# A two-layer hybrid network (SSD mixer, then MLA attention): three projection tiles in step with the input, and group 0's last steps moved into the next group's stream

## The chip, the cores and the metric

The kernel runs on one core of one Trainium2 chip. The metric is the device time of one execution in microseconds (us). A core has five engines that work from instruction streams of their own: PE (matrix products), DVE (vector operations), ACT (activations, copies), POOL and SP; here SP only issues DMAs, and POOL does nothing that matters. Within its stream an engine works in order: an instruction that waits for another engine holds up all that stands behind it.

## The reference

Sequence 512, width 1024, two layers with residuals, fp32. Layer 0 is an SSD (state space) mixer, layer 1 an MLA attention mixer:

```python
u = rms_norm(h, norm_w[0])
proj = u @ in_w                                  # 2048 z + 4096 xbc + 32 dt columns
xbc = silu(causal_depthwise_conv(xbc, conv_w, conv_b))      # 4 taps
dt = softplus(dt_raw + dt_bias);  a = -dt * exp(a_log)
# 8 groups of 4 heads, chunks of 128 tokens:
cb      = C_t . B_s                               # per group and chunk
y_diag  = (cb * exp(a_cum[t] - a_cum[s]), s <= t) @ (x * dt)
states  = B^T @ (x * dt * exp(a_end - a_cum));  carried over chunks
y_off   = (C @ entering_state) * exp(a_cum)
y = (y_diag + y_off + D * x) * silu(z)
h = h + (group_rms_norm(y) * norm_w) @ out_w
# layer 1: MLA mixer (low-rank q and kv, rope, 16 heads, gate silu(z)), then the final rms_norm
```

The change touches layer 0 alone.

## The kernel before

Everything is kept transposed, 128 channels on the partitions by 512 tokens. A product of full precision is made of three fp32r products: each operand is split into a high part (an ACT cast: `whi`, `vh`, `ah`) and the rest (a DVE subtraction: `wlo`, `vl`, `al`), and high by high, low by high and high by low are added in PSUM. So one projection tile (128 output channels) is 8 steps over the input channels of 3 products, 24 products of 128x512.

**Weights.** One tile's weights are 128x1024 fp32 (512 KB). SP loads them in the table's order into two `raw` buffers; ACT writes `whi`, DVE writes `wlo` (three buffers each). When a tile is asked for, the split of the tile after it has just been put into the streams (LOOK is 1).

**The first tiles.** The input x comes in 8 pieces of 256 KB, the first two weight tiles in quarters between them. `gemm2` (L300) makes the B and C tiles of group 0 together, step by step. These first products take x before its norm (`vh`, `vl`); the factor 1/rms comes from a sum of squares and two products with a matrix of ones (`pssq`, L356, L357), an Ln and an Exp on ACT, three DVE steps (`rr`), and it is multiplied in when the PSUM tiles are taken out (L606).

**Groups.** `ssm_in(g)` makes six tiles for group g: B, C, x0, x1, z0, z1 (called B1, C1 ... for group 1). Each is followed by its evacuation: for B, C and x an ACT pass (L608) and three DVE taps of the convolution (L610), and silu on ACT once all are there. The SSD work of a group has steps: `lexp` (four `L` rows are loaded from DRAM by SP, ACT and DVE subtract, ACT takes the exponent), `cb` (transposes of B, L71, and C by B, L77; the result is multiplied into the L tiles by DVE), `x(0)` and `x(1)` (transposes of x, L89, then `xdt` and `xw` on DVE), `states` (L105, then the carry `S` on DVE) and `y` (L130 into `yo`, L138 into `yd`, then DVE). There are four L buffers: the L rows of the next group are loaded when `yd` of this one has read them. `gnorm` is the gated norm of a group's y: squares, `pssq` products, Ln, Exp, DVE.

**What sets the order.** PE's stream is written out by hand: `sched` runs the six tiles of group g+1 and drops the steps of group g between them, at the positions of a table (in us of product time since the start of that stream): `P0` for group 0's steps in the stream of group 1, `P1` for all later ones, `GN` for the gated norm of the group before. The ACT and DVE streams are set by a scheduler that works on what PE's order asks for. On ACT, all uses of the exp/ln table (`E`) and of the silu table (`S`) are kept in phases that alternate; the table load stands between them, and a phase begins only when the one before it is through.

Of the kernel before, what the change touches and what calls it, by code (L numbers as in the profile page):

```python
# [15 lines left out]
P = 128  # L16
T = 512
# [19 lines left out]
S0P = (13.82, 14.2, 15.4, 15.6, 17.62)  # L37
SU = (0.64, 1.42)
P0 = (6.0, 6.8, 11.91, 15.25, 17.25, 24.88, 34.5)
# [12 lines left out]
SQ = 2  # L52

# [98 lines left out]
class Net:  # L152
# [123 lines left out]

    def mm(self, n=T):
        return self.ps.tile([P, n], F32, tag="mm", name=self.nm("mm"), bufs=3)
# [16 lines left out]
    def gemm2(self, ps, ws, xh, xl, ks):  # L295
        seqs = [self.passes(w, xh, xl, ks) for w in ws]
        for k in range(ks):
            for p, seq in zip(ps, seqs):
                for i in range(3 * k, 3 * k + 3):
                    self.nc.tensor.matmul(p, seq[i][0], seq[i][1], start=i == 0, stop=i == 3 * ks - 1)  # L300
            yield 6 * 0.216
# [35 lines left out]
    def sumsq(self, tiles, n, pstag, pool=None, tags=("r0", "rt", "rr"), after=None):  # L337
        nc = self.nc
        acc = None
        for x in tiles:  # L340
            sq = self.nrm.tile([P, T], F32, tag="sq", name=self.nm("sq"), bufs=SQ)
            i = nc.scalar.activation(sq[:], x, AF.Square)
            if after is not None:
                self.link(i, [after])
# [15 lines left out]
    def ssm(self):  # L360
# [10 lines left out]
        self.phase, self.group = "E", [self.head]  # L371
        raws = [self.wraw.tile([P, D], F32, tag="raw", name=self.nm("raw")) for _ in range(2)]
        self.wload = 2
        for k in range(KD):
            x = self.res.tile([P, T], F32, tag="res", name=self.nm("x"))
            nc.sync.dma_start(x[:], t["x"][k])
            self.xs.append(x)
            if k % 2 == 0:
                s = slice(k * P, (k + 2) * P)
                for i, raw in enumerate(raws):  # L380
                    nc.sync.dma_start(raw[:, s], t["w"][i, :, s])
# [11 lines left out]
        vh, vl = [], []  # L393
        ws = [self.split_weight(raw, (256, 512, 768)) for raw in raws]
        for k in range(KD):
            a = self.o16.tile([P, T], F32R, tag="o", name=self.nm("vh"))
            b = self.o16.tile([P, T], F32R, tag="o", name=self.nm("vl"))
            last = nc.scalar.activation(a[:], self.xs[k][:], AF.Copy, scale=nw[:, k:k + 1])
# [9 lines left out]
        self.wpos = 2  # L408
# [24 lines left out]
        for g in range(NG):  # L433
            ys, q = [], []
            pieces = [] if g == 0 else [(GN, late)]
            if g == 0:
                begin = lambda: q.append(SSD(self, 0, self.lexp(0), ys))
                pieces += [(SU[0] + SU[1] * k, scaled) for k in range(KD)]
                pieces += [(P0[0], step), (P0[1], step), (P0[1] + 0.1, begin)]
                at = P0[2:]  # L440
            else:
                q.append(SSD(self, g, self.lexp(g), ys))
# [122 lines left out]
    def ssm_in(self, g, uh, ul, early):  # L565
# [3 lines left out]
        for i, (name, ct) in enumerate((("B", 16 + g), ("C", 24 + g), ("x0", 2 * g), ("x1", 2 * g + 1),  # L569
                                        ("z0", 0), ("z1", 0))):  # L570
            pair = (0, 1) if g == 0 and i < 2 else (4, 5) if g == NG - 1 and i >= 4 else None
            w = None if pair and i == pair[1] else self.weight("w", U_IN + 6 * g + i)
# [5 lines left out]
            if pair:  # L578
                if i == pair[0]:
                    two = [ps, self.mm()]  # L580
                    ws = [w, self.weight("w", U_IN + 6 * g + i + 1)]
                    yield from self.gemm2([p[:] for p in two], ws, xh, xl, KD)
# [489 lines left out]
```

## Time and profile before

| | |
|---|---|
| median of 3 runs | 840.51 us (840.49 to 840.99) |
| the profiled execution | 840.15 us, span of its instructions 838.3 us |
| PE busy | 822.8 us (98%) |
| DVE busy | 640.2 us (76%) |
| ACT busy | 453.5 us (54%) |
| HBM read, written | 83.12 MB, 4.33 MB |

The span is what the profiler saw from the first instruction to the last; 1.85 us of the execution lie around it. In the rows, PE's products are pipelined: a row's length is longer than the distance to the next row, and the distance is the rate. An entry in square brackets is the idle time of the engine just before an instruction, and what ended it.

### The profile page before, as it was taken

Reading aid. Unit: us, or ns where it says so; the run is one execution under the profiler, and the core shown is the slowest. Engines: PE = TensorE matmul, PEld = TensorE weight load, DVE = VectorE, ACT = ScalarE, POOL = GpSimd, SP = SyncE. Lnnn points to the kernel's source line nnn. Section 1 sums busy time; section 2 is a strip of 40 time slices with the busy share of each in tenths; the row PEclk is TensorE's granted clock in tenths of the full one; section 3 lists DMA queues with packets and bytes.
Section 4 is the critical chain, followed back from the end, with each engine's and each line's share of the span. In section 5 each row is a group of like instructions: output and inputs, shape, how many; then the busy total and the mean of one; then the engine's idle time right before and its main releaser. Section 6 shows DMA issues by size and latency. Waiting matters only on the chain.

```text
span 838.3 us, 11586 instructions
## 1 busy us (share of the span) xinstructions
PE 822.8 (98%) x4260; PEld 694.8 (83%) x4260; DVE 640.2 (76%) x1226; ACT 453.5 (54%) x802; POOL 0.2 (0%) x4
## 2 busy tenths in 40 slices
PE   7999999999999999999999999999999999999996
PEld 5887888888888888888888888888888888888885
DVE  7899898979788979776564887786767869675544
ACT  7567755545565657333354664456547557554233
POOL 0000000000000000000000000000000000000000
PEclk9999999999999999999999999999999999999999
DMA  6354543434242424323225242222221224331212
GB/s 227 102 186 145 153 150 106 147 101 128 98 151 76 151 87 137 121 95 101 90 86 176 79 129 64 77 65 73 73 64 56 89 75 157 100 100 53 92 59 100
DMA packets 35112, 90.55 MB, mean 108 GB/s; under 512 B 4784, under 2 KB 6320, under 8 KB 35056
## 3 DMA queue, kind: packets, MB, share of 16 engines
q1 hardware_dynamic: 34336, 88.77, 32.9%
q10 hardware_dynamic: 720, 1.05, 0.3%
q8 instruction: 33, 0.54, 0.3%
q14 instruction: 23, 0.19, 0.1%
HBM read 83.12 MB, written 4.33 MB: 104 GB/s over the span
## 4 chain that ended last, share of the span: by engine, by line
PE 91%; DVE 5%; DMA 2%; ACT 1%; issue 1%; SPq 0%; DVEq 0%; ACTq 0%
PE mm L291 54%; PE ot L942 11%; PE s L794 5%; PE mm L300 4%; PE po L836 4%; PE mm L774 3%; PE pt L818 2%; PE yd L138 2%; PE yd L291 1%; PE aux L130 1%; PE aux L105 1%; DMA x<-in_x_dram 1%; PE aux L77 1%; PE aux L89 1%; DMA L<-ac_d 1%; DVE wlo L273 1%
## 5 line engine op out<-in xcount | busy, mean ns | idle before, releaser
L272 ACT CAST whi<-raw 128x1024 fp32r<-128x1024 f32 (+3 forms) x132 | 127.0, 965 | 214.7 <-PE mm L291 177.4
L273 DVE TENSOR_TENSOR wlo<-raw,whi 128x1024 fp32r<-128x1024 f32 (+3 forms) x132 | 146.8, 1115 | 56.1 <-ACT whi L272 55.8
L291 PE MATMUL mm<-ah,whi 128*128 128x512 f32 x384 | 153.9, 401 | 0.0
L291 PE MATMUL mm<-ah,wlo 128*128 128x512 f32 x384 | 150.1, 391 | 0.4 <-DVE wlo L273 0.4
L291 PE MATMUL mm<-al,whi 128*128 128x512 f32 x384 | 149.8, 390 | 0.0
L291 PE MATMUL mm<-vh,whi 128*128 128x512 f32 x224 | 89.6, 400 | 0.9 <-ACT whi L272 0.9
L291 PE MATMUL mm<-vh,wlo 128*128 128x512 f32 x224 | 87.8, 392 | 0.7 <-DVE wlo L273 0.7
L291 PE MATMUL mm<-vl,whi 128*128 128x512 f32 x224 | 87.5, 391 | 0.0
L291 PEld LDWEIGHTS mm<-ah,wlo 128*128 128x128 f32 x384 | 72.1, 188 | 16.0 <-DVE wlo L273 0.8
L291 PEld LDWEIGHTS mm<-ah,whi 128*128 128x128 f32 x384 | 72.2, 188 | 15.5 <-issue 1.4
L291 PEld LDWEIGHTS mm<-al,whi 128*128 128x128 f32 x384 | 72.2, 188 | 14.4 <-DVE al L312 0.3
L942 PE MATMUL ot<-whi,ah 128*128 128x512 f32 (+1 forms) x136 | 52.3, 384 | 0.0
L942 PE MATMUL ot<-whi,al 128*128 128x512 f32 (+1 forms) x136 | 51.4, 378 | 0.0
L942 PE MATMUL ot<-wlo,ah 128*128 128x512 f32 (+1 forms) x136 | 51.4, 378 | 0.0
L291 PEld LDWEIGHTS mm<-vh,wlo 128*128 128x128 f32 x224 | 42.0, 188 | 10.8 <-DVE wlo L273 1.5
L291 PEld LDWEIGHTS mm<-vh,whi 128*128 128x128 f32 x224 | 42.1, 188 | 9.2 <-ACT whi L272 1.1
L223 ACT ACTIVATE p<-p,st 128x128 f32<-128x128 f32 (+1 forms) x64 | 36.1, 564 | 25.1 <-DVE st L806 25.0
L291 PEld LDWEIGHTS mm<-vl,whi 128*128 128x128 f32 x224 | 42.2, 188 | 7.2
L822 ACT CAST ph<-pt 128x512 fp32r<-128x512 f32 (+1 forms) x64 | 26.5, 422 | 33.2 <-PE pt L818 32.8
L291 PE MATMUL mm<-ch,whi 128*128 128x512 f32 x104 | 42.6, 409 | 0.0
L291 PE MATMUL mm<-ch,wlo 128*128 128x512 f32 x104 | 40.8, 392 | 0.0
L291 PE MATMUL mm<-cl,whi 128*128 128x512 f32 x104 | 40.7, 392 | 0.0
(225 smaller groups left out, 1642.6 us busy)
## 6 DMA issues: line engine op xcount, KB each, us to landing
raw<-in_w_dram SPq DMA_DIRECT2D x100, 512.0 KB, 3.3
L<-ac_d SPq DMA_DIRECT2D x32, 256.0 KB, 3.8
E<-ea_d SPq DMA_DIRECT2D x32, 128.0 KB, 3.3
raw<-in_ua_dram SPq DMA_DIRECT2D x8, 512.0 KB, 3.3
raw<-in_ub_dram SPq DMA_DIRECT2D x8, 320.0 KB, 2.9
x<-in_x_dram SPq DMA_DIRECT2D x8, 256.0 KB, 4.3
res<-in_x_dram SPq DMA_DIRECT2D x8, 256.0 KB, 3.3
hd<-ht SPq DMA_DIRECT2D x8, 256.0 KB, 2.3
```

What stands on the lines that cost most here:

```text
L138: nc.tensor.matmul(yd[64 * h:64 * h + 64, s], self.xdt[j][:, c, h, :], self.L[2 * j + h][:, s], start=True, stop=True)
L223: i = self.nc.scalar.activation(out, in_, func, **k)
L272: nc.scalar.copy(hi[:, a:b], raw[:, a:b])
L273: nc.vector.tensor_tensor(lo[:, a:b], raw[:, a:b], hi[:, a:b].bitcast(F32), op=ALU.subtract)
L291: self.nc.tensor.matmul(ps, a, b, start=i == 0, stop=i == len(seq) - 1)
L300: self.nc.tensor.matmul(p, seq[i][0], seq[i][1], start=i == 0, stop=i == 3 * ks - 1)
L774: nc.tensor.matmul(ps[:, c2 * 256:(c2 + 1) * 256], a, b, start=i == 0, stop=i == 5)
L794: nc.tensor.matmul(ps[:, :n], x[:, s], y[:, :n], start=k == 0, stop=k == 4)
L818: nc.tensor.transpose(pt[:, (b - kb) * P:(b - kb + 1) * P], probs[h][b][:, kb * P:(kb + 1) * P], self.ident)
L822: nc.scalar.copy(ph[:, :n], pt[:, :n])
L836: nc.tensor.matmul(po[:, kb * P:], x, y, start=kb == 0 and k == 0, stop=kb == NCH - 1 and k == 2)
L942: nc.tensor.matmul(ps[:, a:b], x, y, start=start and i == 0, stop=stop and i == 5)
```

## The change

- Eight products of a zero matrix with itself (128x128, fp32) stand at the head of PE's stream; DVE clears the matrix first.
- Three weight tiles, not two, come in quarters with x: group 0's B, C and x0 are made together, step by step. The third tile's raw weights lie in two `act` buffers for that time. SP issues 12 quarters between the 8 pieces of x. The splits of the three tiles (`split_first`) stand between the casts of x.
- The squares of x for the norm are released one by one (after the cast of the piece three further on) and no more after the last cast.
- The four first steps of the table (dt products, norm, the multiplication by `rr`, evacuation) all stand behind the three tiles, at 15.5; the dt transposes follow the fourth tile.
- In the stream of group 1 (`ssm_in(1)`), group 0's steps stand later: `a4` 12.5 (6.0 before), `lexp` 14.1 (6.9), `cb` 19.4 (11.91), `x` 22.5 and 24.0 (15.25, 17.25). Its `states` and `y` (24.88 and 34.5 before) leave that stream: they are now at 2.0 and 7.0 of the stream that makes group 2's tiles, where group 1's own steps move back to 12.0 to 27.0 (1.0 to 18.2 before), and group 0's gated norm to 29.5 (16.84). From the stream of group 3 on the table is as it was.

```diff
-S0P = (13.82, 14.2, 15.4, 15.6, 17.62)
+S0P = (15.5, 15.51, 15.52, 15.53, 24.2)
-P0 = (6.0, 6.8, 11.91, 15.25, 17.25, 24.88, 34.5)
+P0 = (12.5, 14.0, 19.4, 22.5, 24.0)
+PL = (2.0, 7.0)
+PM = (12.0, 13.4, 14.8, 21.0, 27.0)
+GM = 29.5
+WARM = 8
...
+    def split_first(self, raw):
+        nc = self.nc
+        hi = self.whi.tile([P, D], F32R, tag="hi", name=self.nm("whi"))
+        lo = self.wlo.tile([P, D], F32R, tag="lo", name=self.nm("wlo"))
+        for k, part in enumerate(raw):
+            s = slice(2 * k * P, 2 * (k + 1) * P)
+            nc.scalar.copy(hi[:, s], part)
+            nc.vector.tensor_tensor(lo[:, s], part, hi[:, s].bitcast(F32), op=ALU.subtract)
+            yield
+        yield hi, lo
...
+        nc.vector.memset(idle[:], 0.0)
+        pw = aux()
+        for _ in range(WARM):
+            nc.tensor.matmul(pw[:, :P], idle[:], idle[:], start=True, stop=True)
         raws = [self.wraw.tile([P, D], F32, tag="raw", name=self.nm("raw")) for _ in range(2)]
+        third = [self.act.tile([P, T], F32, tag=g, name=self.nm("raw")) for g in ("ah", "al")]
...
-            pss = self.sumsq([x[:] for x in self.xs], D, "aux", after=last)
+            pss = self.sumsq([x[:] for x in self.xs], D, "aux", after=[marks[min(k + 3, KD - 1)] for k in range(KD)])
...
-            pieces = [] if g == 0 else [(GN, late)]
+            pieces = [] if g == 0 else [(GM if g == 1 else GN, late)]
+            elif g == 1:
+                pieces += [(PL[0], lambda: first[0].states()), (PL[1], lambda: first[0].y()), (PL[1] + 0.1, begin)]
+                at = PM
...
-            pieces += [(at[0], lambda: q[0].cb()), (at[1], lambda: q[0].x(0)), (at[2], lambda: q[0].x(1)),
-                       (at[3], lambda: q[0].states()), (at[4], lambda: q[0].y())]
+            pieces += [(at[0], lambda: q[0].cb()), (at[1], lambda: q[0].x(0)), (at[2], lambda: q[0].x(1))]
+            if g:
+                pieces += [(at[3], lambda: q[0].states()), (at[4], lambda: q[0].y())]
...
-            pair = (0, 1) if g == 0 and i < 2 else (4, 5) if g == NG - 1 and i >= 4 else None
+            pair = (0, 1, 2) if g == 0 and i < 3 else (4, 5) if g == NG - 1 and i >= 4 else None
```

Lines of the changed kernel are higher by 4 to 28 than those of the same code before. Three places of the streams that result:

PE's stream from its head, where the zero products now stand (`vh_`, `vl_` are the parts of x; `whi_`, `wlo_` with one number belong to one weight tile). Before:

```order
L300 MATMUL mm_184<-vh_130,whi_133 128x512
L300 MATMUL mm_184<-vl_131,whi_133 128x512
L300 MATMUL mm_184<-vh_130,wlo_134 128x512
L300 MATMUL mm_185<-vh_130,whi_137 128x512
L300 MATMUL mm_185<-vl_131,whi_137 128x512
L300 MATMUL mm_185<-vh_130,wlo_138 128x512
L300 MATMUL mm_184<-vh_142,whi_133 128x512
```

Now:

```order
L391 MATMUL aux_97<-idle 128x128 x8
L315 MATMUL mm_209<-vh_147,whi_150 128x512
L315 MATMUL mm_209<-vl_148,whi_150 128x512
L315 MATMUL mm_209<-vh_147,wlo_151 128x512
L315 MATMUL mm_210<-vh_147,whi_154 128x512
L315 MATMUL mm_210<-vl_148,whi_154 128x512
L315 MATMUL mm_210<-vh_147,wlo_155 128x512
L315 MATMUL mm_211<-vh_147,whi_158 128x512
L315 MATMUL mm_211<-vl_148,whi_158 128x512
L315 MATMUL mm_211<-vh_147,wlo_159 128x512
L315 MATMUL mm_209<-vh_163,whi_150 128x512
```

A step over the input channels is now nine products and not six.

DVE's stream ahead of the weights of tile B2, the first tile of group 2 (its `wlo` is 841 before and 849 now). Before:

```order
L94 TENSOR_TENSOR xw_645<-xdt_770,dec 128x3x128
L610 SCALAR_TENSOR_TENSOR x_132_731<-raw_732,cols,x_132_731 128x509
L606 TENSOR_TENSOR raw_786<-mm_752,rr_311 128x512
L273 TENSOR_TENSOR wlo_795<-raw_746,whi_794 128x1024
L109 COPY S_830<-aux_825 128x256
L610 SCALAR_TENSOR_TENSOR x_142_785<-raw_786,cols,x_142_785 128x511
L112 TENSOR_TENSOR S_832<-S_830,dec 128x256
L610 SCALAR_TENSOR_TENSOR x_142_785<-raw_786,cols,x_142_785 128x510
L113 TENSOR_TENSOR S_832<-aux_825,S_832 128x256
L610 SCALAR_TENSOR_TENSOR x_142_785<-raw_786,cols,x_142_785 128x509
L112 TENSOR_TENSOR S_835<-S_832,dec 128x256
L273 TENSOR_TENSOR wlo_841<-raw_792,whi_840 128x1024
```

Now:

```order
L638 SCALAR_TENSOR_TENSOR x_130_735<-raw_736,cols,x_130_735 128x511
L638 SCALAR_TENSOR_TENSOR x_140_790<-raw_791,cols,x_140_790 128x511
L638 SCALAR_TENSOR_TENSOR x_130_735<-raw_736,cols,x_130_735 128x510
L638 SCALAR_TENSOR_TENSOR x_140_790<-raw_791,cols,x_140_790 128x510
L638 SCALAR_TENSOR_TENSOR x_130_735<-raw_736,cols,x_130_735 128x509
L638 SCALAR_TENSOR_TENSOR x_140_790<-raw_791,cols,x_140_790 128x509
L96 TENSOR_TENSOR xdt_821<-aux_816,dt 128x512
L96 TENSOR_TENSOR xdt_835<-aux_830,dt 128x512
L98 TENSOR_TENSOR xw_728<-xdt_821,dec 128x3x128
L98 TENSOR_TENSOR xw_728<-xdt_835,dec 128x3x128
L277 TENSOR_TENSOR wlo_849<-raw_797,whi_848 128x1024
```

From the multiplication of the dt tile by `rr` (L500, now L528) to this row, DVE's stream holds the same instructions as before less four of group 0's carry `S` and one `wlo`, which stands ahead of `rr` now.

ACT's stream at the silu of group 2 (its B is 1013 before and 929 now; `r_210`, `r_230` are the Ln and Exp of group 0's gated norm). Before:

```order
L608 ACTIVATE C_1049<-mm_1024,cols 128x512
L353 CAST sqh_1125<-sqa_1118 128x512
L272 CAST whi_1209<-raw_1103 128x1024
L608 ACTIVATE x_199_1098<-mm_1060,cols 128x512
L223 ACTIVATE r_210_1132<-pssq_1129 128x512
L223 ACTIVATE r_210_1132<-r_210_1132 128x512
L232 ACT_TABLE_LOAD
L232 ACTIVATE B_1013<-B_1013 128x512
L232 ACTIVATE C_1049<-C_1049 128x512
```

Now:

```order
L660 ACTIVATE L_1300<-L_1300,ac 128x128
L660 ACTIVATE L_1300<-L_1300,ac 128x128 x3
L357 ACTIVATE sq_1497<-y_1238 128x512
L227 ACTIVATE r_230_1276<-pssq_1273 128x512
L357 ACTIVATE sq_1501<-y_1243 128x512
L227 ACTIVATE r_230_1276<-r_230_1276 128x512
L641 COPY z_233_1292<-mm_1199 128x512
L236 ACT_TABLE_LOAD
L236 ACTIVATE B_929<-B_929 128x512
L236 ACTIVATE C_1037<-C_1037 128x512
```

The Ln, Exp and silu of that phase now stand behind the last tile of group 2 and behind the first `L` row of group 2's own exponents (`L_1300`), which is loaded after group 1's `yd` products.

More of the change, by code (lines that the diff above doesn't have):

```diff
@@ L371, in ssm @@
         self.phase, self.group = "E", [self.head]
+        idle = wk.tile([P, P], F32, name="idle", bufs=1)
+        nc.vector.memset(idle[:], 0.0)
+        pw = aux()
+        for _ in range(WARM):
+            nc.tensor.matmul(pw[:, :P], idle[:], idle[:], start=True, stop=True)
         raws = [self.wraw.tile([P, D], F32, tag="raw", name=self.nm("raw")) for _ in range(2)]
-        self.wload = 2
+        raws = [[raw[:, 2 * k * P:2 * (k + 1) * P] for k in range(KD // 2)] for raw in raws]
+        third = [self.act.tile([P, T], F32, tag=g, name=self.nm("raw")) for g in ("ah", "al")]
+        raws.append([third[k // 2][:, (k % 2) * 2 * P:(k % 2 + 1) * 2 * P] for k in range(KD // 2)])
+        self.wload = 3
         for k in range(KD):
@@ L579, in ssm_in @@
                 if i == pair[0]:
[L580 to L581 removed]
+                    two = [ps] + [self.mm() for _ in pair[1:]]
+                    ws = [w] + [self.weight("w", U_IN + 6 * g + k) for k in pair[1:]]
                     yield from self.gemm2([p[:] for p in two], ws, xh, xl, KD)
```

23 lines of the change are left out of this document (12 added, 11 removed).

## The prediction

> **What bounds the kernel now.** First the page's span and busy times, then the list of what PE waited for, then PE's rows in order of time at its gaps.
>
> ```profile
> span 838.3 us, 11586 instructions
> PE 822.8 (98%) x4260; PEld 694.8 (83%) x4260; DVE 640.2 (76%) x1226; ACT 453.5 (54%) x802; POOL 0.2 (0%) x4
> ```
>
> PE, 98% busy, sets the time. Its waits after 90 us, the whole list, are two of 0.2 us:
>
> ```profile
> PE mm L291 <- ACT whi L272: 0.2, 1, 0.2
> PE mm L291 <- DVE wlo L273: 0.2, 1, 0.2
> ```
>
> So what is to be won lies before 90 us, and whatever the change makes PE wait later is new. PE's rows there:
>
> ```profile
> 4.77 0.80 PE L300 MATMUL mm<-vh,whi 128*128 128x512 f32 x1 [4.77 <-ACT whi L272]
> ...
> 7.99 0.63 PE L300 MATMUL mm<-vl,whi 128*128 128x512 f32 x1
> 8.42 0.63 PE L300 MATMUL mm<-vh,wlo 128*128 128x512 f32 x1
> ...
> 11.29 0.39 PE L300 MATMUL mm<-vl,whi 128*128 128x512 f32 x1
> 11.52 0.39 PE L300 MATMUL mm<-vh,wlo 128*128 128x512 f32 x1
> ...
> 18.69 0.50 PE L291 MATMUL mm<-vh,whi 128*128 128x512 f32 x1 [0.66 <-ACT whi L272]
> 19.95 0.50 PE L291 MATMUL mm<-vh,wlo 128*128 128x512 f32 x1 [0.53 <-DVE wlo L273]
> ...
> 24.88 0.39 PE L357 MATMUL pssq<-sql,onesr 128*128 128x512 f32 x1
> ...
> 29.53 0.66 PE L504 MATMUL aux<-ident,d 128*128 128x128 f32 x4 [0.16 <-DVE d L500]
> 29.94 0.48 PE L291 MATMUL yd<-vh,whi 128*128 128x512 f32 x1
> ...
> 78.69 1.56 PE L105 MATMUL aux<-xw,BT 128*128 128x256 f32 x6 [0.87 <-DVE xw L94]
> 81.08 0.50 PE L291 MATMUL mm<-ah,wlo 128*128 128x512 f32 x1 [0.37 <-DVE wlo L273]
> 86.25 1.50 PE L130 MATMUL aux<-C,S 128*128 128x128 f32 x12
> 87.68 1.97 PE L138 MATMUL yd<-L,xdt 128*64 128x128 f32 x32
> 131.52 1.06 PE L77 MATMUL aux<-C,B 128*128 128x128 f32 x8
> ```
>
> Read the distances: the first ten products are 0.43 us apart, later ones 0.227. The third tile waits 1.19 us for its weights; near 80 us PE waits 1.24 us for DVE. I measure everything against 131.52, `cb` of group 2: from there PE's stream is the same in both kernels.
>
> **The opening.** One row of the table by stretches (length; busy time of PE, weight loads, DVE, ACT, POOL; clock; DMA share; GB/s), then rows of ACT, DVE and the chain that pace the first products:
>
> ```profile
> 5.18:12.70 7.52, 7.52 (x26) 5.93 (x26) 6.38 (x13) 6.50 (x13) 0.00 (x0) 1.00 1.01 355
> 6.22 0.72 ACT L398 ACTIVATE vh<-x,nw 128x512 fp32r<-128x512 f32 x1 [0.63 <-DMA x<-in_x_dram]
> 4.46 0.75 DVE L402 SCALAR_TENSOR_TENSOR vl<-x,nw,vh 128x512 fp32r<-128x512 f32 x1 [3.54 <-ACT vh L398]
> 8.52 4.18 DMA x<-in_x_dram
> ```
>
> Between 5.18 and 12.70 the DMA engines are full (share 1.01) at 355 GB/s, and the last x lands at 12.70. Four more quarters of 131 KB are 0.52 MB, 1.5 us: the last x lands near 14.2. That is early enough, since PE now has 72 products to make, 16.3 us. Only the second step waits: its x has one quarter more ahead of it, 0.37 us, and lands at 6.59; 0.72 for `vh` and 0.75 for `vl` make 8.1, when the first step's nine products have long been made at full rate (4.77 to about 6.9). From the second product of step two 62 are left: 8.1 + 62 x 0.227 = 22.2. The dt products and `pssq` are 18 more: PE begins tile x1 at **26.3**, where it began it at 29.94 with the dt transposes (0.41) done: **3.2 us won**. The bounds: 25.2, if nothing waits (90 products from 4.77), and 27.3, if the first step stays slow (nine products of 0.43 end at 8.6, and some more).
>
> That last case is the zero products' part. A 128x128 fp32 product costs as much as a 128x512 one here (four in 0.82 us at 62.14), so eight at half rate fill some 3.5 us, from DVE's first clear near 1.0 to about 4.5: they cover idle time. [...]
>
> Rows of PE, DVE and ACT, and a second stretch:
>
> ```profile
> 62.14 1.06 PE L77 MATMUL aux<-C,B 128*128 128x128 f32 x8
> 29.18 1.05 ACT L272 CAST whi<-raw 128x1024 fp32r<-128x1024 f32 x1 [2.61 <-PE mm L291]
> 30.13 0.81 ACT L608 ACTIVATE B<-raw,cols 128x512 f32<-128x512 f32 x1
> 28.78:85.40 56.62, 55.23 (x261) 45.19 (x260) 54.34 (x96) 37.64 (x62) 0.00 (x0) 1.00 0.42 133
> 84.26 1.22 DVE L273 TENSOR_TENSOR wlo<-raw,whi 128x1024 fp32r<-128x1024 f32 x1
> ```
>
> **Stall 1, the weights of B2.** `rr` still needs `pssq`, so DVE starts its long work (d, with which the stretch at 28.78 begins, 3.7 after the second `pssq`) at 30.0 now: later than before, while PE is 3 us ahead. From d to B2's `wlo` (84.26) DVE is busy 54.34 us in the row by stretches. The new stream has the same instructions but for four carries S (about 1.5) and one `wlo` (1.14): 51.7. And ACT, in order, casts B1's weights ahead of B's pass; the buffer comes free at the end of tile x1, 5.4 after its start; cast and pass are 1.8 more (29.18 to 30.93), so the first tap starts at 26.3 + 7.2, and DVE idles 1.2. Its d and three evacuations (2.4) lie ahead of that. So B2's `wlo` is ready at 26.3 + 7.2 + 49.3 = **82.8**. PE, without a wait: from 29.94 to 86.25 it took 56.3, of which the waits (1.24) and the states (1.4) fall away and the transposes (0.45) come in: 54.1, and two products: 26.3 + 54.6 = 80.9. **PE waits 1.9** (1.2 to 3.2: small idle times, or `whi` casts that come earlier). Before, the same `wlo` had 4.6 us to spare (85.40 against 90.0), because PE made states and y first.
>
> **Stall 2, the weights of z0 of group 2.** The L rows of group 1 can be loaded only when `yd` of group 0 is made, and that now stands late:
>
> ```profile
> 88.80 2.13 SPq L627 DMA_DIRECT2D L<-ac_d  x4
> 93.99 1.57 ACT L632 ACTIVATE L<-L,ac 128x128 f32<-128x128 f32 x5 [1.91 <-DMA L<-ac_d]
> 99.60 0.77 ACT L608 ACTIVATE B<-mm,cols 128x512 f32<-128x512 f32 x1
> 101.36 0.68 DVE L92 TENSOR_TENSOR xdt<-aux,dt 128x512 f32<-128x512 f32 x1
> 101.96 0.74 DVE L610 SCALAR_TENSOR_TENSOR B<-mm,cols,B 128x511 f32<-128x511 f32 x1
> 102.62 0.55 DVE L94 TENSOR_TENSOR xw<-xdt,dec 128x384 f32<-128x384 f32 x1
> 103.09 0.74 DVE L610 SCALAR_TENSOR_TENSOR B<-mm,cols,B 128x510 f32<-128x510 f32 x1
> L<-ac_d SPq DMA_DIRECT2D x32, 256.0 KB, 3.8
> ```
>
> From B2's `wlo` PE makes ten products, states, 24 products and the first half of y: 2.3 + 1.4 + 5.5 + 2.4; first `yd` at 94.4. Load 0.2 + 3.8 (median; 5.2 in the rows at 88.80); the relus and exponents took 5.6 (93.99 to 99.60); behind them on ACT stands C2's pass, 0.8: 104.8. DVE waits for that, and then makes six taps of C and x (0.66 each by the distances of the rows), three multiplications of L and two `xdt` (0.60), two `xw` (0.47) and `wlo` of z0 (1.22): 9.1, ready at **113.9**. PE would be there at 94.4 + 17.3 (the second `yd` 0.95, 62 products 14.2, `cb` 1.2, transposes 0.9): 111.7. **PE waits 2.2** (0.6 to 3.3, for a load of 2.8 to 5.2).
>
> **Stall 3, the silu of group 2.** Silu of B2 and C2 may follow only the Ln and Exp of group 0's norm, now at the end of that stream, 12 products ahead of group 2's `cb`, which needs both:
>
> ```profile
> 111.57 0.60 ACT L223 ACTIVATE r<-pssq 128x512 f32<-128x512 f32 x1 [0.33 <-PE pssq L357]
> 112.20 0.63 ACT L223 ACTIVATE r<-r 128x512 f32<-128x512 f32 x1
> 112.86 1.28 ACT L232 ACT_TABLE_LOAD   x1
> 114.15 0.63 ACT L232 ACTIVATE B<-B 128x512 f32<-128x512 f32 x1
> ```
>
> Before, that chain ended 16 us ahead of 131. Now it has a square (0.53) and z1's copy (0.5) in it as well: from the second `pssq` product 0.4 + 0.63 + 0.53 + 0.63 + 0.5 + 1.3 + 1.1 = 5.1, against 3.4 until PE wants C. So 1.8 at least. Ahead of Ln also stand the relus of group 2's first L row (1.27) and a square; its load begins 3.9 before `pssq` (group 1's first `yd`), takes 3.8, and Ln starts 1.8 after `pssq`, not 0.4: 1.4 more. **PE waits 3.1** (1.8 to 4.6). In time: z0 at 113.9, first `yd` of group 1 10.2 later (four products, states, 24 products, half of y), `pssq` 4.0 later at 128.1, `cb` of C at **134.6**, against 131.52.
>
> **Sum.** Won: 3.2 + 1.24 = 4.4. Paid: 1.9 + 2.2 + 3.1 = 7.2. Net 2.8, or 3.1 by the running time (134.6 - 131.5); I take 3.1, which rounds less. The profiled execution was 840.15, so 843.25; the median lies 0.36 above it: **843.6 us**. All bounds that favour it: 3.6 of waits less 5.5 won, 838.6; all that do not: 11.1 less 3.4, 848.2.
>
> **Rivals.** *DVE keeps up (faster).* Stall 1 and 2 rest on sums within 2 us of PE's arrival. If ACT and DVE run some 2 us shorter to B2 and z0, only stall 3's floor is left: 1.8 less 4.4, 837.9. For it: the old order left DVE 2.3 us idle in that stretch (56.62 against 54.34); against: these are left out of my sum already, and the new order has a wait of its own at the first tap. It decides if `wlo` of B2 comes before 81. *No change.* L loads of 3 us and a tighter DVE: 0.9 + 0.9 + 2.4 against 4.4, 840.4. For it: the shortest x load took 2.8; against: L's median is 3.8. *The clock falls back.* The opening shows that ten products at half rate cost 2.0 us; if a wait of 3 us lets the rate fall again, that is added per stall, 845.6 for one, 847.6 for two. [...] *The zero products do not warm the array:* 1.0 more, 844.6.
>
> **Chances.** A measurement of this kernel can tell about 0.2%, 1.7 us. Forecast 0.41 (842.2 to 846 by itself), colder clock 0.07, no warming 0.05: slower 0.53. No change 0.27. DVE keeps up, faster: 0.20. The forecast's margin over that 1.7 us is small against its bounds, hence the large chance of no change. The range reaches past the faster case's 837.9, halfway to the 836 of a stream without any wait (840.5 less 4.4): 837.0 to 847.0.
>
> **What would show it.** Right: products at 0.227 apart from the first real ones; tile x1 begins at 25.5 to 27; PE rows with a wait for DVE `wlo` at B2's third product near 81, the same at z0 near 112, and a wait for ACT's silu at `cb` near 131, of 2 to 3 us each; DVE idle for about 1 us just ahead of the first tap of B. Wrong: if PE runs from 30 to 130 without these waits, the time is near 836; if the opening ends after 27.3, x came later than the rate says.

## The result: slower by 6.4 us, and where the profile after shows it

The changed kernel took **847.02 us** (median of 4 runs, 845.79 to 848.38) against 840.57 before: ratio 1.0076, with a 95% interval of 1.0059 to 1.0094. The prediction said 843.6, with a range up to 847.0, at whose end the median lies; the direction and its three waits were right, and the size was about half of what came. The profiled execution of the changed kernel took 847.61, with a span of 845.8, 7.5 more than before. One execution of the runs below, of the kernel with the moved steps alone, took 3455 us, at a granted clock listed as 1.0; nothing here explains it, and no time below includes it.

The page's span and busy times, then the list of what PE waited for:

```profile
span 845.8 us, 11623 instructions
PE 829.9 (98%) x4276; PEld 700.5 (83%) x4276; DVE 640.9 (76%) x1230; ACT 452.4 (53%) x805; POOL 0.2 (0%) x4
...
PE mm L306 <- DVE wlo L277: 4.9, 3, 3.3
PE aux L75 <- ACT B L236: 2.5, 1, 2.5
```

PE is busy 7.1 us more than before, though eight zero products (16 rows of the trace, 3.8 us) are all the work that was added, and it fills time that was idle. So waits alone are not the loss: some of the products took longer. PE's rows at the head, at the start of tile x1 and at the three new waits show both:

```profile
1.04 3.78 PE L391 MATMUL aux<-idle 128*128 128x128 f32 x16 [1.04 <-DVE eps L346]
...
4.88 0.69 PE L315 MATMUL mm<-vh,whi 128*128 128x512 f32 x1
...
6.04 0.40 PE L315 MATMUL mm<-vh,whi 128*128 128x512 f32 x1
6.28 0.39 PE L315 MATMUL mm<-vl,whi 128*128 128x512 f32 x1
...
26.90 0.40 PE L306 MATMUL yd<-vh,whi 128*128 128x512 f32 x1
...
80.80 0.39 PE L306 MATMUL mm<-al,whi 128*128 128x512 f32 x1
84.48 0.79 PE L306 MATMUL mm<-ah,wlo 128*128 128x512 f32 x1 [3.29 <-DVE wlo L277]
85.07 0.63 PE L306 MATMUL mm<-ah,whi 128*128 128x512 f32 x1
85.50 0.63 PE L306 MATMUL mm<-al,whi 128*128 128x512 f32 x1
...
88.91 2.32 PE L109 MATMUL aux<-xw,BT 128*128 128x256 f32 x6
90.88 0.58 PE L306 MATMUL mm<-ah,whi 128*128 128x512 f32 x1
...
117.89 0.50 PE L306 MATMUL mm<-ah,wlo 128*128 128x512 f32 x1 [1.44 <-DVE wlo L277]
118.22 0.40 PE L306 MATMUL mm<-ah,whi 128*128 128x512 f32 x1
118.46 0.40 PE L306 MATMUL mm<-al,whi 128*128 128x512 f32 x1
...
137.74 0.55 PE L75 MATMUL aux<-ident,B 128*128 128x128 f32 x3 [2.50 <-ACT B L236]
138.26 1.95 PE L81 MATMUL aux<-C,B 128*128 128x128 f32 x8
...
142.25 0.60 PE L93 MATMUL aux<-ident,x 128*128 128x128 f32 x4
```

Read the distances again. The first two real products at the head are 0.52 apart; the next ones, up to a short wait for `vl` at 8.59, are 0.22 to 0.38 apart where they were 0.43. Tile x1 begins at 26.90 (29.94 before). Behind the wait of 3.29 us the products are 0.43 apart and the states take 1.97 us, until 90.88, and `cb`'s products behind the wait of 2.50 take 1.60 us to the next row where they took 0.81; behind the wait of 1.44 the distance is 0.23 at once. The table by stretches, whose last three columns are granted clock, DMA share and GB/s, says the same:

```profile
84.48:91.30 6.82, 6.82 (x17) 5.38 (x18) 1.51 (x3) 1.88 (x2) 0.00 (x0) 0.55 0.47 155
...
137.74:142.01 4.27, 4.27 (x16) 3.63 (x17) 3.57 (x7) 4.25 (x7) 0.00 (x0) 0.60 0.01 2
```

So the account, against the rows of before: PE is due at B2's third product at 81.03 (80.80 and one step of 0.227). Before, that product stood at 90.15, with group 0's states (1.11) and y (3.33) ahead of it, which now come later: 85.7. Won by then: 4.7. Lost: three waits, 3.68 + 1.84 + 2.89 from the start of the row ahead (80.80, 116.05, 134.85) less three steps of 0.227, 7.7; half rate from 84.48 to 90.88, 3.0 (ten distances that sum to 4.43 where 2.27 would do, and states 1.97 for 1.11); half rate behind 137.74, 1.9 (from there to the transposes of x 4.51, where 131.19 to 133.81 took 2.62 before). That makes 7.7 + 3.0 + 1.9 - 4.7 = 7.9; the transposes of x stand 8.4 later than before (142.25 against 133.81), and PE's last product 8.2 later. The rest, 0.5, has no row of its own and stays unexplained.

What held DVE and ACT back, in rows of both:

```profile
27.03 1.05 ACT L276 CAST whi<-raw 128x1024 fp32r<-128x1024 f32 x1 [3.09 <-DMA raw<-in_w_dram]
27.99 0.59 ACT L227 ACTIVATE r<-pssq 128x512 f32<-128x512 f32 x1
28.11 1.23 DVE L277 TENSOR_TENSOR wlo<-raw,whi 128x1024 fp32r<-128x1024 f32 x1 [2.65 <-ACT whi L276]
...
31.45 0.69 DVE L528 TENSOR_TENSOR d<-aux,rr 128x512 f32<-128x512 f32 x1
34.13 0.75 DVE L638 SCALAR_TENSOR_TENSOR B<-raw,cols,B 128x511 f32<-128x511 f32 x1 [0.20 <-ACT B L636]
83.20 2.36 DVE L277 TENSOR_TENSOR wlo<-raw,whi 128x1024 fp32r<-128x1024 f32 x2
131.95 1.28 ACT L660 ACTIVATE L<-L,ac 128x128 f32<-128x128 f32 x4 [5.58 <-DMA L<-ac_d]
133.65 0.58 ACT L227 ACTIVATE r<-pssq 128x512 f32<-128x512 f32 x1
...
137.05 0.63 ACT L236 ACTIVATE B<-B 128x512 f32<-128x512 f32 x1
```

ACT stands at the cast of the weights of group 0's z1, the sixth tile (the expectations below call it the fifth), until they land at 27.03, with the norm's Ln behind it; DVE then makes that tile's `wlo` ahead of `rt`. So `d` starts at 31.45, and from there to B2's `wlo` (ready at 84.4) DVE is idle 0.6 us in all. At 131.95 ACT stands at group 2's first L row with group 0's Ln behind it, and silu of B ends at 137.7.

### The profile page after: what moved, and what is told of

Its sections match the earlier page's. It is cut to its first block, busy times and chain, and to the rows that moved or that the text cites. A ratio compares the mean times of both kernels' runs of the same rounds, so it can differ in the third digit from the quotient of the medians.

```text
span 845.8 us, 11623 instructions
## 1 busy us (share of the span) xinstructions
PE 829.9 (98%) x4276; PEld 700.5 (83%) x4276; DVE 640.9 (76%) x1230; ACT 452.4 (53%) x805; POOL 0.2 (0%) x4
## 4 chain that ended last, share of the span: by engine, by line
PE 87%; DVE 8%; DMA 2%; ACT 2%; issue 1%; SPq 0%; ACTq 0%; DVEq 0%
PE mm L306 49%; PE ot L970 10%; PE mm L315 6%; PE s L822 5%; PE po L864 4%; PE mm L802 3%; PE pt L846 2%; PE yd L142 2%; PE aux L109 1%; PE aux L134 1%; DVE x L638 1%; DVE wlo L277 1%; DMA L<-ac_d 1%; PE aux L81 1%; DVE C L638 1%; PE yd L306 1%
## 5 line engine op out<-in xcount | busy, mean ns | idle before, releaser
L276 ACT CAST whi<-raw 128x1024 fp32r<-128x1024 f32 (+2 forms) x123 | 123.1, 1002 | 219.3 <-PE mm L306 164.8
L277 DVE TENSOR_TENSOR wlo<-raw,whi 128x1024 fp32r<-128x1024 f32 (+2 forms) x123 | 142.5, 1161 | 59.4 <-ACT whi L276 59.1
L306 PE MATMUL mm<-vh,whi 128*128 128x512 f32 x216 | 86.1, 399 | 0.0
L306 PE MATMUL mm<-vh,wlo 128*128 128x512 f32 x216 | 84.6, 391 | 0.2 <-DVE wlo L277 0.2
L306 PE MATMUL mm<-vl,whi 128*128 128x512 f32 x216 | 84.3, 390 | 0.0
```

Source lines behind the costliest of these rows:

```text
L276: nc.scalar.copy(hi[:, a:b], raw[:, a:b])
L277: nc.vector.tensor_tensor(lo[:, a:b], raw[:, a:b], hi[:, a:b].bitcast(F32), op=ALU.subtract)
L306: self.nc.tensor.matmul(ps, a, b, start=i == 0, stop=i == len(seq) - 1)
```

## The experiments

The runs of the kernel before beside them had medians of 840.32 to 840.52.

**Is the half rate the idle time's doing?** Zero products fill the two waits; all other streams stay as they are.

```diff
+                if g == 2 and i == 0:
+                    for _ in range(F2):                  # 14
+                        nc.tensor.matmul(ps[:, :P], self.idle[:], self.idle[:], start=True, stop=True)
...
+        if self.g == 2:
+            for _ in range(F3):                          # 6, ahead of the transposes of B
+                nc.tensor.matmul(pb[:, :P], net.idle[:], net.idle[:], start=True, stop=True)
```

> The changed kernel (847.0) with zero products where PE waits: 14 ahead of tile B2 (14 x 0.2 = 2.8 us of a wait of 3.29) and 6 ahead of the transposes of group 2's B (1.2 of 2.50). All other streams are as in the changed kernel. If PE falls to half rate because it stood idle (products 0.43 apart after 84.48 and after 137.74, which cost 2.9 and 1.9 us there), the idle stretches are now about 0.5 to 1 and 1.3 us, the products behind them stay 0.227 apart, and the time is 847.0 - 4.8 = 842.2. If the half rate has another cause (power, or the place in the program), or if the waits are all there is, the time stays at 847.0, or rises by as much as the zero products run over the waits.

Measured: 843.75 (842.72 to 848.0), ratio 1.0043 (1.0026 to 1.0061), 3.3 less than the changed kernel; 842.2 was expected. PE's rows of the profiled execution (848.0, the longest of the seven):

```profile
80.68 3.29 PE L621 MATMUL mm<-idle 128*128 128x128 f32 x28
...
84.04 0.40 PE L311 MATMUL mm<-al,whi 128*128 128x512 f32 x1
84.27 0.41 PE L311 MATMUL mm<-ah,wlo 128*128 128x512 f32 x1
...
115.58 0.54 PE L311 MATMUL mm<-ah,wlo 128*128 128x512 f32 x1 [2.35 <-DVE wlo L282]
115.92 0.63 PE L311 MATMUL mm<-ah,whi 128*128 128x512 f32 x1
...
138.12 0.55 PE L80 MATMUL aux<-ident,B 128*128 128x128 f32 x3 [2.21 <-ACT B L241]
...
139.93 0.63 PE L311 MATMUL mm<-al,whi 128*128 128x512 f32 x1
140.36 0.63 PE L311 MATMUL mm<-ah,wlo 128*128 128x512 f32 x1
```

With PE kept at work over the first wait, the products behind it are 0.23 apart: `wlo` comes at nearly the same time (DVE's row begins at 82.90, 83.20 in the changed kernel), and the half rate is gone. That shows the cause there. But the gain is handed on in part: PE comes 3 us earlier to z0 of group 2, waits 2.35 there in place of 1.44, and now that wait is followed by half rate. At the third place six products were too few in this execution. In five of the seven the mean granted clock was 0.997 or 0.998, as in the kernel before (0.996 to 0.998); it was 0.994 in this one and 0.991 to 0.996 in the changed kernel's four. By that clock most executions had little or no half rate left.

**Does the third wait come from the norm's place?** Two places for group 0's gated norm.

```diff
-GM = 29.5
+GM = 18.0        # first run;  27.05 in the second
```

> The changed kernel with group 0's gated norm at 18.0 of the stream that makes group 2, not at 29.5. If the wait of 2.50 us for silu of group 2 comes from the norm's place at the end (the Ln behind the L rows that land at 131.95), it goes, with the half rate behind it: 847.0 - 2.5 - 1.9 = 842.6. If the silu is late for another reason (the weights and the copies of its own tiles), the time stays at 847.0. If the six norm steps that now stand on DVE ahead of x1's taps of group 2 make the next weights late, a wait of 1 to 3 us comes up at z1 or y, near 122 to 128, and the time is 844 to 846.

Measured at 18.0: 850.28 (848.9 to 851.66), ratio 1.0111 (1.0094 to 1.0128), 3.3 more. The wait for silu is gone from PE's list, but the norm's sum stands where its squares are not summed yet:

```profile
119.88 0.80 PE L371 MATMUL pssq<-sqh,onesr 128*128 128x512 f32 x1 [8.18 <-ACT sqh L368]
```

DVE made the steps of the sum of squares only behind group 1's `xw` and two tiles' weights (116.96 and 118.49), so PE waited 8.2 us, and half rate followed. None of the outcomes written down was this one; the run shows only that the norm can also stand too early.

> The changed kernel with group 0's gated norm right behind group 1's y (27.05 in place of 29.5): its two sums on PE stand 12 products earlier, and Ln and Exp on ACT now ahead of group 2's L rows; up to there all streams are as in the changed kernel. Theory: the wait for silu (2.50 us, then 1.9 of half rate) goes, the two earlier ones stay: 847.0 - 4.4 = 842.6. Rival: silu is held by something else (the table load's phase, the z copies), and the wait stays above 2 us: 847.

Measured at 27.05, right behind group 1's y: **842.89** (839.74 to 844.0), ratio 1.0023 (1.0013 to 1.0032); 842.6 was expected. The whole list of PE's waits over 0.3 us, but for the one at its head:

```profile
PE mm L306 <- DVE wlo L277: 4.9, 3, 3.3
```

The third wait is gone, and with it the half rate behind it: 4.1 us of the change's 6.4 hang on 12 products' difference in the place of a norm. Its Ln now runs at 128.27, ahead of the L rows.

**What are the zero products worth?** One in place of eight; nothing else moves.

```diff
-WARM = 8
+WARM = 1
```

> The changed kernel with one zero product in place of eight, nothing else moved. If the eight products make PE fast in time, the first nine or ten real products are now 0.43 apart and the time goes up by at most 1.0 us at the start of tile x1 (847.0 to 848.0), less where step two waits for x anyway. DVE's long work starts at 31.45 behind rr, which follows pssq; if that moves by as much, the wait at B2 stays 3.3 us; if rr is held by something else (the cast of the fifth tile's weights), B2's wlo comes at the same time and nothing is lost at all: 847.0.

Measured: 848.25 (844.89 to 849.96), ratio 1.0087 (1.0063 to 1.0112): no difference from the changed kernel that the intervals show. The rows do show what the eight do:

```profile
7.72 0.63 PE L315 MATMUL mm<-vh,whi 128*128 128x512 f32 x1
8.15 0.63 PE L315 MATMUL mm<-vl,whi 128*128 128x512 f32 x1
...
27.40 0.40 PE L306 MATMUL yd<-vh,whi 128*128 128x512 f32 x1
...
136.65 0.55 PE L75 MATMUL aux<-ident,B 128*128 128x128 f32 x3 [2.89 <-ACT B L236]
...
138.40 0.40 PE L306 MATMUL mm<-al,whi 128*128 128x512 f32 x1
138.63 0.39 PE L306 MATMUL mm<-ah,wlo 128*128 128x512 f32 x1
```

The first products are 0.43 apart again, tile x1 begins 0.5 later, and B2's weights come at the same time (84.50 against 84.48): the later start is made up for the most part by a shorter wait there (2.96 against 3.29).

**Which half of the change brings the waits?** The opening with group 0's states, y and norm and group 1's steps back in their old streams, and the moved steps alone (old opening).

```diff
-P0 = (12.5, 14.0, 19.4, 22.5, 24.0)
+P0 = (12.5, 14.0, 19.4, 22.5, 24.0, 30.0, 34.5)
...
-            pieces = [] if g == 0 else [(GM if g == 1 else GN, late)]
+            pieces = [] if g == 0 else [(GN, late)]
...
-            elif g == 1:
-                pieces += [(PL[0], lambda: first[0].states()), (PL[1], lambda: first[0].y()), (PL[1] + 0.1, begin)]
-                at = PM
```

> The new opening with group 0's states and y back at the end of group 1's stream, the norm of group 0 at 16.84 and group 1's own steps at their old places; only group 0's steps before the states keep the new places, because the new opening makes DVE start its long work 2.7 us later while PE is 3.0 earlier. Theory: the wait for B2's wlo (3.3 and 2.9 of half rate), the one for z0 of group 2 (1.4) and the one for silu (2.5 and 1.9) come from the moved states and y, and go; what is left is a wait of 1.5 to 2 us for xw at group 0's states (83.2 against PE's 81.3). Of 4.1 us won some 2 remain: 838 to 839. Rival: the opening's lag of DVE alone costs what the opening wins, a wait of 3 us or more ahead of the states with half rate behind it: 840.5 to 843.

Measured: 842.10 (841.0 to 842.8), ratio 1.0019 (1.0010 to 1.0028): neither the 838 to 839 of the theory nor faster than before. PE waits at group 0's states and at its y, 4.5 us in all:

```profile
83.07 1.53 PE L109 MATMUL aux<-xw,BT 128*128 128x256 f32 x6 [2.60 <-DVE xw L98]
...
87.60 1.16 PE L134 MATMUL aux<-C,S 128*128 128x128 f32 x8 [1.51 <-DVE S L117]
88.69 3.58 PE L142 MATMUL yd<-L,xdt 128*64 128x128 f32 x32
```

and the `yd` products behind it take 3.5 us to the next row where they took 1.9. The time is the rival's, but the run is not quite the opening alone: at 30.0 the states stand right ahead of y, where the kernel before had 24 products between the two. DVE has to make S in between, so the waits for S (0.43 and 1.51) go with that place; with twelve products between, in the last two runs below, at most 0.2 of them is left. What the opening's lag of DVE does by itself is at most the 2.60 for xw. With these places, the opening costs more than it wins.

> The kernel before with only the second half of the change: group 0's states, y and gated norm in the stream that makes group 2, group 1's steps moved back; the old opening and the old places of group 0's first steps. Theory: the waits for xw and wlo (1.24) go; PE reaches B2's third product near 84.1, its wlo is ready near 84: no or a small wait there; the wait for z0 of group 2 (1.4 to 2.4) and the one for silu (2.2 to 2.5) come with the move, each with up to 1.9 of half rate: 840.5 - 1.24 + 5.5 = 844.8 (843.5 to 846.5). Rival: the waits come from the opening's lead of PE over DVE; then the move alone is 839.3.

Measured: 849.43 (846.78 to 850.95, three executions), ratio 1.0101 (1.0078 to 1.0124): slower than the theory's upper end of 846.5. Its waits are those of the run that follows.

> The kernel of the run with only the moved steps (old opening), whose profile could not be read, once more for its waits. It measured 846.8 to 851 against 844.8 expected. Theory: besides the waits at z0 of group 2 (1.4 to 2.4) and silu (2.2 to 2.5) there is one at B2's wlo of 1 to 3 us, since nothing but the order of work changed there, each of 2 us or more with half rate behind it: the waits sum to 6 to 8 us. Rival: one wait of another kind (the L rows' load, a table) of over 4 us.

Measured: 851.81 (851.28 and 852.33), ratio 1.0135 (1.0117 to 1.0154). PE's rows at its waits, and the row of ACT ahead of the last:

```profile
81.88 0.79 PE L294 MATMUL mm<-ah,wlo 128*128 128x512 f32 x1 [3.44 <-DVE wlo L276]
...
142.56 0.90 PE L74 MATMUL aux<-ident,B 128*128 128x128 f32 x3 [4.52 <-ACT B L235]
...
136.78 1.28 ACT L640 ACTIVATE L<-L,ac 128x128 f32<-128x128 f32 x4 [7.60 <-DMA L<-ac_d]
```

With one of 1.69 at z0 of group 2 these are three waits, 9.7 us, as the theory had it, but larger, and the first stands one tile earlier than it said: at the weights of z1 of group 1, since without the states ahead of it PE reaches that tile 2.3 us earlier (78.05 against 80.32 for the product ahead of the wait). The last is over 4 us, and ahead of it ACT stands 7.60 us at the L rows, so the rival is right in part. So each half, with these places of the table, is slower than the kernel before, the moved steps by far the more; the whole change costs less than the moved steps alone, and which of the opening's edits gives that back was not tried.

**Is DVE's late start the first wait's cause?** The dt products are split so that the first norm's sums stand behind four of them, in the changed kernel and in the opening alone.

```diff
             nc.tensor.matmul(ps[:], lhs, vl[k][:], start=False, stop=k == KD - 1)
+            if k == 1:
+                yield
...
-                   list(zip(S0P, (step, norm0, step, self.flush, step))))
+                   list(zip(S0P, (step, norm0, step, step, self.flush, step))))
```

> The changed kernel with the sums for the first norm placed behind the first four of the 16 dt products, not behind all: PE has them 2.0 us earlier (it waits some 0.5 for DVE's half of the sum), rr follows, and on DVE the cast of the fifth tile's weights falls behind rr. Theory: DVE is the bound from rr to B2's weights, 53 us without a gap, so d starts near 28.3 in place of 31.45, B2's wlo is there 3 us earlier, the wait at B2 falls from 3.3 to under 1 us, and its half rate (2.9) goes. PE then comes 6 us earlier to group 2, where the wait at z0 grows to 2.4 with some half rate, as in the run with zero products, and the one for silu stays: 847.0 - 6 + 1.5 = 842 to 843. Rival: not DVE's start but a later wait on the way (dt's chain, casts of weights) sets B2's wlo: the wait at B2 stays near 3.3, 846 to 847.

Measured: 843.46 (841.51 to 845.49), ratio 1.0035 (1.0023 to 1.0047): 3.6 less than the changed kernel, just above the theory's 842 to 843; its rival, 846 to 847, falls.

> The new opening alone (as in the run before with states and y at their old places, 842.1) with the first norm's sums behind the first four dt products. That run waited 4.5 us for DVE's xw and S at group 0's states, and lost some 1.5 to half rate behind it. Theory: DVE starts 3 us earlier, the waits fall to 1.5 or less and the half rate goes: 838 to 839, faster than the kernel before. Rival: the steps between (dt's chain, L rows, the E and silu phases of ACT) do not come earlier with rr, and PE waits there instead: 841 to 842.

Measured: 839.82 (838.93 to 842.56), ratio 0.9996 (0.9987 to 1.0005): no change from the kernel before, between the theory and its rival. Rows of DVE and PE, of the changed kernel with early `rr` and then of the opening alone with it:

```profile
28.59 0.69 DVE L530 TENSOR_TENSOR d<-aux,rr 128x512 f32<-128x512 f32 x1
70.71 0.87 DVE L664 TENSOR_SCALAR L<-L,ac 128x128 f32<-128x128 f32 x4 [1.25 <-DMA L<-ac_d]
83.14 0.50 PE L306 MATMUL mm<-ah,wlo 128*128 128x512 f32 x1 [1.44 <-DVE wlo L277]
```

```profile
71.21 0.88 DVE L661 TENSOR_SCALAR L<-L,ac 128x128 f32<-128x128 f32 x4 [2.32 <-DMA L<-ac_d]
84.21 2.90 PE L109 MATMUL aux<-xw,BT 128*128 128x256 f32 x6 [3.53 <-DVE xw L98]
```

`d` starts 2.9 earlier, and B2's weights come 1.3 earlier, not 3. Of the rest 1.14 goes to the `wlo` of z1 of group 0, which stood ahead of `d` and now stands behind it, and 1.25 to the L rows, at which DVE now runs dry, since their place in the table had been set for the late start. In the first kernel that was enough to leave no half rate at B2. So the start of DVE's long work is a cause, and behind it the table's places are the next one. The run does not tell `d` from B's pass on ACT: the edit also puts that pass ahead of the cast of B1's weights (29.91 and 33.00; 33.29 and 32.33 in the changed kernel), and in the changed kernel DVE's first tap waited 0.20 for it.

**Versions that follow from this.** Early `rr`, the norm at 27.05 and earlier places for a4 to x (first run); the opening alone with early `rr` and such places (second and third).

```diff
-P0 = (12.5, 14.0, 19.4, 22.5, 24.0)
+P0 = (9.0, 10.0, 16.0, 19.5, 21.0)                    # with GM = 27.05
```

> The changed kernel with three edits: the first norm's sums behind the first four dt products, the norm of group 0 right behind group 1's y, and group 0's a4, lexp, cb and x steps earlier (9.0, 10.0, 16.0, 19.5, 21.0), since with rr early DVE has a4's input 6 us before PE took it and then waited 1.25 us for the L rows. Theory: the wait at B2 falls from 1.44 to about 0.5, the one at z0 stays at 1.4 to 1.7, the one for silu goes (2.6 and some 1.7 of half rate): 843.5 - 1 - 4.3 = 838.2, faster than the kernel before by 2. Rival: DVE's total work from rr to z0 of group 2 binds, so that z0's wait takes what B2's loses: 840.

Measured: 842.76 (841.92 to 843.32), ratio 1.0029 (1.0019 to 1.0039); 838.2 was expected, and it is above the rival's 840 too. DVE has no gap at the L rows any more, but the weights of z1 of group 1 now stand behind six taps of x, and PE, which came to that tile at 75.6, waits there:

```profile
79.43 0.50 PE L306 MATMUL mm<-ah,wlo 128*128 128x512 f32 x1 [3.62 <-DVE wlo L277]
```

> The new opening with early rr, states and y of group 0 at their old places in the stream of group 1 (28.0 and behind its end), and a4, lexp, cb and x at 9.0, 10.0, 16.0, 18.5 and 19.5; on DVE xw of x1 now stands ahead of B2's weights. Theory: DVE's gap of 2.3 us at the L rows closes and xw comes at 79 in place of 84.2; PE waits 1 us or less there, no half rate: 839.8 - 3.2 - 1.5 = 835 to 837. Rival: what is taken from that wait comes back at S, the second half of y or B2's weights, behind which DVE's work stands now: 839.

The places were 9.0, 10.0, 16.0, 18.5, 19.5, 28.0 and 34.5; at 28.0 twelve products stand between the states and y, 24 in the kernel before. Measured: **838.80** (837.64 to 839.51), ratio 0.9978 (0.9969 to 0.9987): faster than the kernel before, less than hoped. One wait is left, of 1.92 us, for z1's weights.

> The kernel of the run before (the new opening, early rr, states and y at their old places, 838.80) with one number changed: group 0's x(1) at 21.2 in place of 19.5, so that one xdt (0.60) falls behind the weights of z1 on DVE, for which PE waited 1.92. Theory: DVE's order just ahead of those weights is what is left of the bound; the wait falls by 0.6 to 1.3, xw still comes before the states: 838.2. Rival: xw or S is now late by as much: 838.8.

Measured: **837.84** (837.6 to 838.96), ratio 0.9970 (0.9958 to 0.9982). The time is a little better than the theory's 838.2, but the wait for z1's weights fell by 0.32 only, to 1.60, where 0.6 to 1.3 was expected; the intervals of this run and the one before overlap.

This is the fastest kernel of the study, 2.5 us under the one before. It keeps the change's opening and drops its moved steps; the early `rr` and the new places are not part of the change.

## Why the prediction was right, and where it failed

- **The opening**: right. Tile x1 began at 26.90 (26.3 foreseen, bounds 25.2 to 27.3). Of the 0.6, 0.5 is step two's second product, which began at 8.59 and not at 8.1, since its `vl` came at 8.5. That zero products bring the first step to full rate, as its sum has it, the trace of before does not show; behind the eight its first two products were 0.52 apart and the next 0.22 to 0.38, and with one zero product the first products were 0.43 apart.
- **Stall 1**: right in place and cause, mis-sized: 3.29 for 1.9. `wlo` was ready at 84.4, not 82.8. Of these 1.6 us, 0.6 is the later start of tile x1. The first tap then came 7.2 after that start (34.13), just as foreseen, and from the tap to the end of `wlo` it took 50.3 where the sum had 49.3: a wait of 0.36 for a cast at 52.45, about 0.2 more busy time (49.53), and 0.4 in gaps too short to be listed. "d at 30.0" was wrong as well: it started at 31.45, 0.6 of it from tile x1 and 0.85 from the cast of the sixth tile's weights ahead of Ln on ACT and its `wlo` ahead of `rt` on DVE. That cost nothing at the first tap, which waited for ACT all the same (0.20 idle, 1.2 foreseen). PE's arrival, 81.0 for 80.9, was luck in part: the tile began 0.6 late, and the stretch behind it took 54.1, not 54.6.
- **Stall 2**: 1.44 for 2.2, within its bounds. From the middle of group 0's `yd` (98.9, half of the row at 97.97) PE took the 17.3 foreseen; the weights came some 0.6 sooner than the 19.5 of the sum. No run tests this wait's cause by itself.
- **Stall 3**: 2.50 for 3.1, with the cause foreseen; the run at 27.05 shows it.
- **The sum of the waits** was 7.2 as the page counts them, 7.2 in the prediction; that is luck, since the three are off by +1.4, -0.8 and -0.6. What was won was 4.7 against 4.4. By these terms alone the changed kernel would have been 2.5 us slower (3.0 with the waits counted from row to row), the forecast's 3.1.
- **What failed is the chance of 0.07 for "the clock falls back"**, and its price. Half rate behind two of the three waits cost 3.0 and 1.9 in the profiled execution where the rival had 2.0 each; its time for two stalls, 847.6, is nearest to what came. The run with zero products shows at the first wait that it came with the idle time: with PE kept at work the products behind it were 0.23 apart. The trace of before had no wait over 0.87 after the one of 4.77 at its head, so it did not show what a longer one costs; the chance was small all the same, though the prediction's own forecast held two or three waits of 2 to 3 us: the one price that they had in common was left out of the sum. The range ended at 847.0, below this rival's 847.6 and below the 848.2 of the prediction's own bounds.
- **The rivals "DVE keeps up" and "no change"** fell: DVE was idle 0.6 us between `d` and B2's weights. **"The zero products do not warm the array"** fell too (0.43 between the first products with one, 0.22 to 0.38 from the third on with eight), but what they win there is for the most part lost again at B2.
- The time varies between executions, and the granted clock with it: with the norm at 27.05 one execution took 839.74 at a mean clock of 0.998 and the other nine 841.65 to 844.0 at 0.994 to 0.996. In the changed kernel the shortest of four (845.79) has the highest clock, 0.996, but the longest (848.38) has 0.994 and not the lowest, 0.991, so the clock is not the whole of it.

## What to carry to other kernels

Work that is moved to follow a faster start wins little while another engine's unbroken queue ends last: find the first instruction of that queue, ask what stands ahead of it, and move that first. Price a new wait on TensorE with the half rate behind it: here no wait of up to 1.92 us that stood alone was followed by it, and 13 of the 14 from 2.21 us on were, at some 1.7 us for each 3.41 us at half clock (an estimate, half of 3.41; next section). A wait that cannot be removed can be filled with products on zeros: here those behind the filled wait were 0.23 us apart, 0.43 where it was not filled. A table of places is tuned for one start: when the start moves, the places behind it move the stall to the next tile rather than remove it.

## What the runs showed of the hardware

The rate of TensorE after a wait, from PE's rows of the profiled executions (half rate is the stretch in which products are about 0.43 us apart, or smaller ones take about twice their time):

| kernel | wait, us | half rate behind it, us |
|---|---|---|
| changed kernel | 3.29 / 1.44 / 2.50 | 6.4 / none / 4.0 |
| zero products in the waits | 2.35 / 2.21 | 3.8 / 3.6, beginning 1.5 after the wait's end |
| one zero product | 2.96 / 1.49 / 2.89 | 2.8 / none / **none** |
| norm at 18.0 | 3.27 / 8.18 | 3.3 / 5.3 |
| norm at 27.05 | 3.31 / 1.44 | 3.7 / none |
| early `rr` | 1.44 / 1.67 / 2.56 | none / none / 3.7 |
| the opening without the moved steps | 2.60 / 0.43 / 1.51, within 4.6 us | 3.4, beginning 1.2 after the last wait's end |
| the same with early `rr` | 3.53 | 3.1 |
| moved steps alone | 3.44 / 1.69 / 4.52 | 5.3 / none / 2.8 |
| early `rr`, norm and places | 3.62 / 1.43 | 3.4, beginning 1.5 after the wait's end / none |
| the two fastest | 1.92; 1.60 | none; none |

Where the waits stand apart, none of up to 1.92 us was followed by half rate, and 13 of the 14 from 2.21 to 8.18 were. The length of a wait does not decide it: one of 2.89 was followed by products 0.23 apart at once, one of 1.51 with two others ahead of it by half rate, and the slow stretch began up to 1.5 us after PE had resumed.

The granted clock shows the same stretches. In the changed kernel it is at 0.50 from 83.82 to 90.65 us and from 138.44 to 141.85, 6.83 and 3.41 us, and at 1.00 in the rest of the first 160 us. In four traces that have two such stretches in that time, their beginnings lie a whole number of 3.413 us apart:

| kernel | clock at 0.50 from, us | apart, us |
|---|---|---|
| changed kernel | 83.82 and 138.44 | 54.62, 16 times 3.414 |
| zero products in the waits | 115.90 and 139.80 | 23.90, 7 times 3.414 |
| norm at 18.0 | 84.18 and 114.90 | 30.72, 9 times 3.413 |
| moved steps alone | 80.58 and 142.02 | 61.44, 18 times 3.413 |

Counted off in steps of 3.413 us from the beginning of a stretch at 0.50 (backwards and forwards), the traces give PE's busy time in a step and the clock of the step after it. Some examples:

| kernel | step at full clock, us | PE busy in it, us | clock in the next |
|---|---|---|---|
| changed kernel, first wait | 80.41 to 83.82 | 0.78 | 0.50 |
| changed kernel, second wait | 114.54 to 117.96 | 1.98 | 1.00 |
| changed kernel, third wait | 135.02 to 138.44 | 0.93 | 0.50 |
| one zero product, the wait of 2.89 | 131.81 to 135.22, 135.22 to 138.63 | 1.96, 1.98 | 1.00, 1.00 |
| early `rr`, norm and places | 77.45 to 80.86 | 1.43 | 0.50 |
| the opening without the moved steps | 85.43 to 88.84 | 1.73 | 0.50 |
| moved steps alone | 118.13 to 121.54 | 1.73 | 1.00 |

In the changed kernel's trace, counted off so from about 9 us to the end of the span, 241 steps at full clock have another behind them: three were followed by 0.50, with PE busy for 0.93 us or less, and 238 by 1.00, with 1.9 us or more. In the trace of the kernel before it is one of 242, from 831.80 to 835.22, when PE had no work left; the others had 2.09 us or more. Between these lie the steps of 1.43 and 1.73 in the table, of which one of 1.73 was followed by 1.00. In the long stretch of the changed kernel PE was busy for 2.75 us in the first step, 83.82 to 87.23, and the clock stayed at 0.50; it was busy for all of the second, and the clock was at 1.00 from 90.65 on. So in these traces a step with little work was followed by one at half clock, and if PE is at work through that one, it loses some 1.7 us (an estimate: half of 3.41). The wait of 2.89 fits this: the end of a step cut it into 1.45 and 1.43 us of idle time. The beginnings of the stretches lie elsewhere in each of these traces (83.82, 84.18 and 80.58 at the first wait of three kernels); whether they do so between executions of one kernel too, and make its time vary, was not shown.

The granted clock does not show half rate at the start of the program: before the change the first ten products were 0.43 apart in a stretch that the page lists at 1.00.
